# A state-space mixer and its gated unit: lower parts of three tiles and of the first gate weights moved behind the scan, rounded products first

## The chip, the cores and the metric

One core of a Trainium2 chip runs the whole program in one launch. The metric is the device time of one execution in microseconds. TensorE is called PE in the views, VectorE DVE, ScalarE ACT, GpSimd POOL, and SyncE, which only issues DMAs here, SP. PEld is TensorE's weight load.

## What is computed

Two layers of a streaming encoder over 1088 positions of width 1024 (1024 positions of a prompt, 64 of a sample). Layer 0 is attention and a convolutional feed-forward network. Layer 1, which the change touches, is a diagonal complex state-space mixer with a gated unit, and then another such network. Cut to the mixer, with `u` the normed input in blocks of 64 positions:

```python
xr, xi = einsum(u, bbr), einsum(u, bbi)            # 64 groups of 16 channels, 64 complex states each
_, _, sr, si = associative_scan(_affine_combine, (ar, ai, xr, xi), axis=1)
y = einsum(sr, cr) - einsum(si, ci) + d_skip * h
z = jax.nn.gelu(y)
ag = z @ w_glu + b_glu                             # 1024 -> 2048
out = ag[..., :D_MODEL] * jax.nn.sigmoid(ag[..., D_MODEL:])
```

All inputs and outputs are float32. PE multiplies rounded numbers (fp32r), so an exact product is made of three: a matrix `w` is split into a rounded part `hi` and the rest `lo`, the data `z` likewise into `zh` and `zl`, and `hi*zl + hi*zh + lo*zh` is summed in PSUM (`mm3`, L222 to L226).

## The kernel before

**The mixer** (`ssm`, from L1206). The 64 groups are worked on in pairs, numbered q = 0 to 31. A batch holds two of these (q and q+1), except that 0, 1, 30 and 31 stand alone. A batch is a generator, and `staged` runs several of them interleaved, oldest first, so that each engine has the stages of several batches in its queue. One batch does: PE makes `p1`, the input of the scan (L1258); ACT makes the tables `sc` and `rd` (L1266, L1270); DVE multiplies, adds, scans and multiplies again (L1289, L1294, L1295, L1306, L1309, L1310); PE turns the state into outputs in two PSUM banks (L1318, L1324, with one or two filling matmuls of L231 between); ACT copies them to the tile `ys` (L1332) and the end states to `fin` (L1335). The second multiplication, L1310, is the last that DVE does for a batch. PSUM is a pool of its own in the mixer; it is closed behind it, so the first matmul of the gated unit waits for the last `ys` copy, that of q = 31.

Eight q make one tile of 128 channels, kt = 0 to 7. When its last q is copied, `ys` goes to DRAM (L1339) and comes back transposed as `yf` (L1344). ACT then makes `z` with a GELU (L1359, L1362) and its rounded part `zh` in three blocks of columns (L1368: 384, 384 and 320), and DVE makes the lower part `zl` in three instructions (L1372). Each of these stands in its engine's queue between steps of later batches. `ys`, `yf` and `z` share five buffers (`t4`).

**The weights.** `load_unit` loads 128 x 1024 weights into `raw`, of which there are two buffers, and `split_unit` makes `whl`: the rounded part on ACT and the lower part on DVE, both on L217. The gated unit's first two units (weights of m = 0 for both halves of the product) are loaded within the mixer, at the last batch.

**The gated unit** (from L1405). `tile_(m, b)` is one of 8 tiles of output channels and one of 3 blocks of columns. For m = 0 all products of the first six kt (`k0 = KD - 2`) are made for the three blocks, then those of kt = 6, then those of kt = 7, since z of these two comes last. Then ACT takes the sigmoid and DVE the gate. A side job on POOL and DVE (`sums`) prepares weights of the next network.

**The preparation pool.** `prep2` held three tiles of 128 x 1024 during layer 0, `w`, `tl` and `tp`, for tables of the mixer. Nothing uses them in the mixer.

What sets the order on an engine is a scheduler with a model of time, which takes waits into account, and `self.order(x, y)`, by which x comes behind y on its queue. Each queue then runs strictly in that order.

Of the kernel before, what the change touches and what calls it, by code (L numbers as in the profile page):

```python
# [8 lines left out]
F32 = mybir.dt.float32  # L9
F32R = mybir.dt.float32r  # L10
I32 = mybir.dt.int32
AF = mybir.ActivationFunctionType
# [3 lines left out]
P = 128  # L16
D = 1024
KD = 8
SEQ, DEC, PAST = 1024, 64, 512
T = SEQ + DEC  # L20
BLK = [(0, 384), (384, 384), (768, 320)]
# [13 lines left out]
KH = KF // 2  # L35
PRODUCTS = (("a", 0, 0, 0, 0), ("a", 1, 0, 1, 0), ("s", 0, 0, 1, 1), ("s", 0, 1, 0, 1), ("a", 1, 1, 1, 0), ("s", 1, 1, 0, 0), ("s", 1, 0, 1, 1))
SUMMED = (0, 0, 1, 1, 1, 1, 0)
NC_ = 137
NPR = 32

# [3 lines left out]
class Core:  # L44
# [165 lines left out]
        return self.split_unit(raw)  # L210

    behind = ()

    def split_unit(self, raw):
        nc = self.nc
        w = self.big([P, 2, D], "whl")
        x = nc.scalar.activation(w[:, 0], raw, AF.Copy), nc.vector.tensor_sub(w[:, 1], raw, w[:, 0].bitcast(F32))  # L217
        for u, v in zip(x, self.behind):
            self.order(u, v)
        return w  # L220
# [803 lines left out]
    def ssm_chunk(self, q):  # L1024

        nc, a = self.nc, self.a
        G, V = nc.gpsimd, nc.vector
        gs = slice(4 * q, 4 * q + 4)
        if q == 0:
            z = self.pt([P, 8, 112], "z0")  # L1030
# [24 lines left out]
            o = bass.AP(tensor=o.tensor, offset=o.offset, ap=[o.ap[0], [2 * P + 32, 4], [P, 2], [1, 16]])  # L1055
            nc.scalar.activation(o, self.tq[r, gs, 32:64].rearrange("p g (c j) -> p g c j", c=2), AF.Copy)

        w = self.prep2.tile([P, 4, 2, 16, 8], F32, name="w")
        m = self.pm2()
        m = [m[:, i, :512].rearrange("p (g j s) -> p g j s", j=16, s=8) for i in range(2)]  # L1060
        row = lambda x: x[:, :, :, None].to_broadcast([P, 4, 16, 8])
# [6 lines left out]
        for g in range(4):  # L1068
            for c in range(2):
                x = nc.tensor.matmul(kps[:, :P], self.bd_[:, g, c], ct[:, g, c, 0:8].rearrange("p t i -> p (t i)"),  # L1070
                                     start=g + c == 0, stop=g + c == 4)
                self.order(x, behind)
        kt = self.prep.tile([P, P], F32, name="kt")
# [23 lines left out]
    def ssm_toeplitz(self, q):  # L1097

        nc = self.nc
        tl, tp = (self.prep2.tile([P, 8, P], F32, name=x) for x in ("tl", "tp"))  # L1100
        kd = self.kd
        for s in range(8):
            src = bass.AP(tensor=kd.tensor, offset=kd[8 * q * 16:8 * q * 16 + 1, s].offset, ap=[[240, 16], [3840, 8], [1, P]])
            dst = tl.rearrange("(j s) g f -> j s g f", s=8)[:, s]
            nc.sync.dma_start(dst, src)
        nc.scalar.activation(tp.rearrange("p g (i t) -> p g i t", i=16), tl.rearrange("p g (t i) -> p g i t", i=16), AF.Copy)
        nc.sync.dma_start(self.prm[:, 4 * q:4 * q + 4, OKT:OKT + 256], tp.rearrange("p (g e) f -> p g (e f)", e=2))

    def ssm_prep(self):
        self.prep_ctx = self.tc.tile_pool(name="prep", bufs=1)  # L1110
        self.prep = self.prep_ctx.__enter__()
        self.ssm_small()
        yield
        for q in range(8):
            yield from self.ssm_chunk(q)
            yield
            self.ssm_toeplitz(q)
        self.prep_ctx.__exit__(None, None, None)
# [86 lines left out]
    def ssm(self, after):  # L1205
        nc, tc, a = self.nc, self.tc, self.a  # L1206
        off = PPO
        yd = self.dram.tile([D, 8, NC_], F32, name="yd")
        zh, zl = [None] * 3, [None] * 3
        with tc.tile_pool(name="ss", bufs=1) as sp:  # L1210
# [4 lines left out]
            ps = ps_ctx.__enter__()  # L1215
# [31 lines left out]
            def batch(qs):  # L1247
                t, n, e0 = qs[0] // 2, len(qs), qs[0] % 2
# [16 lines left out]
                for c in range(2):  # L1265
                    x = nc.scalar.activation(sc[:, :, c], pm[:, :, OSI:PRM], AF.Copy, scale=(1.0, -1.0)[c])  # L1266
# [5 lines left out]
                        self.order(x, out[0])  # L1272
                if qs[-1] == 31:
                    self.wsrc.pop(0)
                    for j in range(AHEAD):
                        self.load_ahead(1 + j)
                        self.order(self.loaded, got[15])
                if qs[0] == 2:
                    self.order(self.spill(), self.last_u)
                    us.append(self.ssm_load(2))  # L1280
# [16 lines left out]
                for q in qs:  # L1297
                    if q % 4 == 0 and q < 28:
                        k = q // 4 + 1
# [37 lines left out]
                if qs[-1] % 4 == 3:  # L1337
                    kt = qs[-1] // 4
                    out.append(nc.scalar.dma_start(yd[kt * P:kt * P + P].rearrange("(g i) t c -> (i t) g c", i=16), ys[0]))  # L1339
                    yf = self.t4([P, 8, NC_], "yf")  # L1340

                    if kt < 7:
                        yield
                    x = nc.sync.dma_start(yf, yd[kt * P:kt * P + P])  # L1344
                    yfs.append(x)
                    if t + 6 in got:
                        self.order(x, got[t + 6])
                    if kt < 7:
                        yield
                        yield  # L1350
                    if kt == 6:

                        yield
                    if kt == 7:
                        yield
                        yield
                    z = self.t4([P, T], "z")
                    yv = yf.rearrange("p t c -> p c t")
                    x = nc.scalar.activation(z[:, 0:SEQ].rearrange("p (c t) -> p c t", t=8), yv[:, 0:128], AF.Gelu_apprx_tanh)  # L1359
                    self.order(x, out[0])  # L1360
                    self.order(x, out[-1])
                    x = nc.scalar.activation(z[:, SEQ:].rearrange("p (c t) -> p c t", t=8), yv[:, 129:137], AF.Gelu_apprx_tanh)  # L1362
                    self.order(x, out[0])
                    self.order(x, out[-1])
                    for b, (t0, n_) in enumerate(BLK):
                        if kt == 0:
                            zh[b], zl[b] = self.bt(self.blk, b, "zh", F32R), self.bt(self.blk, b, "zl", F32R)
                        nc.scalar.activation(zh[b][:, kt], z[:, t0:t0 + n_], AF.Copy)  # L1368
                    if kt < 7:
                        yield  # L1370
                    for b, (t0, n_) in enumerate(BLK):
                        x = nc.vector.tensor_sub(zl[b][:, kt], z[:, t0:t0 + n_], zh[b][:, kt].bitcast(F32))  # L1372
                        if kt < 7:
                            self.order(x, adds[-1])
            scans, ends = [], []
            self.staged([batch(x) for x in [[0], [1]] + [[q, q + 1] for q in range(2, 30, 2)] + [[30], [31]]], oldest=True)
            self.behind = out[0], ends[-1]
            fo = sp.tile([P, P], F32, name="fo")
            nc.vector.tensor_add(fo, *(fin[:, i].rearrange("p q c s -> p (q c s)") for i in range(2)))
            nc.gpsimd.dma_start(a["o_st"], fo)  # L1380
# [29 lines left out]
        with self.boundary():  # L1410
            def tile_(m, b):
# [6 lines left out]
                    y[b] = self.bt(self.yp, b, "y")  # L1418
                pa, pb = self.mm_ps("pa"), self.mm_ps("pb")

                def products(ks):
                    for ps, w in ((pb, ws[m][1]), (pa, ws[m][0])):
                        for k in ks:
                            self.mm3(ps[:, :n], w, slice(k * P, (k + 1) * P), zh[b][:, k], zl[b][:, k], k == 0, k == KD - 1)
                k0 = 0
                if m == 0:

                    k0 = KD - 2
                    products(range(k0))
                    yield  # L1430
                products(range(k0, KD - 1))
                yield
# [7 lines left out]
                yield  # L1440

            order = [tile_(m, b) for m, b in self.tail_order(KD, 3)]
            for x in order[:3]:
                next(x)
            for x in order[:3] * 2 + [x for x in order[3:] for _ in range(2)]:
                next(x)
# [162 lines left out]
```

## Time and profile before

| | |
|---|---|
| three runs | 2238.83, 2241.77, 2240.37 us; median 2240.37 |
| profiled execution | 2241.03 us, span of the trace 2239.2 us |
| PE busy | 2191.6 us, 98% of the span |
| DVE busy | 1661.3 us, 74% |
| ACT busy | 1042.3 us, 47% |
| granted PE clock, mean | 0.992 |
| mixer, about 1190 to 1294.4 us | PE busy 93 of 104 us |
| gated unit, 1294.4 to 1511 us | PE busy 216.23 of 216.60 us |

A row of the timeline has the start in us from the start of the span, the time the instruction (or several like it) took, engine, line, operation, output and input, size, and how many; in brackets the idle time of the engine before it and what ended that. Instructions of an engine overlap by some tens of nanoseconds, so distances between starts are the better measure of what one costs. A row of the stretches has the stretch, its length, the busy time of PE, PEld, DVE, ACT and POOL with the instructions in brackets, the granted PE clock as a share of full speed, the DMA share and GB/s.

### The profile page before, as it was taken

The page shows a single profiled execution, that of the slowest core. Times are in us where ns is not written, and L with a number is a line of the kernel's source. Part 1 is how long each engine was busy: PE and PEld are TensorE (multiplying, and loading weights), DVE is VectorE, ACT ScalarE, POOL GpSimd, SP SyncE. Part 2 cuts the span into 40 slices and gives each one's busy share as a digit, 9 for nine tenths or more (in the row PEclk, how much of TensorE's full clock was granted, in tenths as well). Part 3 has the DMA queues.
Part 4 walks back from the last instruction along what each step waited for, and adds up shares of the span by engine and source line. Part 5 has one row for each costly group of instructions (what it writes and reads, how often), then busy time and mean ns, then how long its engine had stood idle before and what let it go on. Part 6 is the DMA issues. An engine that isn't in the chain of part 4 may idle for free.

```text
span 2239.2 us, 35982 instructions
## 1 busy us (share of the span) xinstructions
PE 2191.6 (98%) x13875; PEld 2117.1 (95%) x13875; DVE 1661.3 (74%) x2886; ACT 1042.3 (47%) x1890; POOL 412.8 (18%) x474
## 2 busy tenths in 40 slices
PE   9999999999999999999988899999999999999997
PEld 8987789999999999999986699999999999999997
DVE  8687647989878877767758855597976776676764
ACT  5255747422343342555545641263555455455543
POOL 5322004200032423000200034352010110110000
PEclk9999999999999999999999899999999999999999
DMA  5100015655355565887749888752266686579772
GB/s 197 37 22 29 20 62 158 241 188 202 122 150 173 176 208 187 274 279 236 233 163 339 263 280 294 249 167 75 87 224 229 218 297 226 196 272 314 218 253 97
DMA packets 208123, 428.47 MB, mean 191 GB/s; under 512 B 23312, under 2 KB 114224, under 8 KB 205008
## 3 DMA queue, kind: packets, MB, share of 16 engines
q1 hardware_dynamic: 175648, 326.56, 44.2%
q0 software_dynamic: 23984, 95.12, 11.9%
q10 hardware_dynamic: 8320, 4.49, 0.8%
q8 instruction: 109, 1.79, 0.3%
q14 instruction: 62, 0.51, 0.1%
HBM read 297.75 MB, written 128.37 MB: 190 GB/s over the span
## 4 chain that ended last, share of the span: by engine, by line
PE 32%; DMA 13%; DVE 9%; issue 4%; ACT 2%; POOL 2%; SPq 0%; DVEq 0%; ACTq 0%; POOLq 0%
PE mm L224 10%; PE mm L226 10%; PE mm L225 10%; DMA sj<-in_w_up 3%; DMA raw<-in_w_down 2%; DMA jw<-in_w_down 2%; DMA raw<-sd 1%; POOL sj L1391 1%; DMA yd<-ys 1%; DVE whl L217 1%; DMA su<-sj 1%; DMA gd<-t 1%; DVE gt L564 1%; DVE t L425 1%; DMA yf<-yd 1%
## 5 line engine op out<-in xcount | busy, mean ns | idle before, releaser
L224 PE MATMUL mm<-hl,whl 128*128 128x384 f32 (+1 forms) x1960 | 643.3, 329 | 4.1 <-DVE hl L307 3.1
L226 PE MATMUL mm<-hh,whl 128*128 128x384 f32 (+1 forms) x1960 | 641.2, 329 | 2.3 <-DVE whl L217 2.3
L225 PE MATMUL mm<-hh,whl 128*128 128x384 f32 (+1 forms) x1960 | 643.1, 328 | 0.0
L224 PEld LDWEIGHTS mm<-hl,whl 128*128 128x128 f32 x1960 | 368.4, 188 | 6.5 <-DVE hl L307 4.7
L226 PEld LDWEIGHTS mm<-hh,whl 128*128 128x128 f32 x1960 | 368.4, 188 | 3.0 <-DVE whl L217 2.9
L225 PEld LDWEIGHTS mm<-hh,whl 128*128 128x128 f32 x1960 | 368.6, 188 | 0.1
L217 DVE TENSOR_TENSOR whl<-raw,whl 128x1024 fp32r<-128x1024 f32 x202 | 254.9, 1263 | 146.7 <-ACT whl L217 146.2
L217 ACT ACTIVATE whl<-raw 128x1024 fp32r<-128x1024 f32 x202 | 213.0, 1058 | 248.1 <-PE mm L226 128.6
L224 PE MATMUL mm<-gt,whl 128*128 128x384 f32 (+1 forms) x968 | 316.8, 327 | 2.9 <-ACT whl L217 2.4
L226 PE MATMUL mm<-gt,whl 128*128 128x384 f32 (+1 forms) x968 | 315.8, 327 | 0.7 <-DVE whl L217 0.7
L225 PE MATMUL mm<-gt,whl 128*128 128x384 f32 (+1 forms) x968 | 315.9, 327 | 0.0
L224 PEld LDWEIGHTS mm<-gt,whl 128*128 128x128 f32 x968 | 181.7, 188 | 3.7 <-ACT whl L217 2.6
L226 PEld LDWEIGHTS mm<-gt,whl 128*128 128x128 f32 x968 | 181.7, 188 | 1.2 <-DVE whl L217 1.2
L225 PEld LDWEIGHTS mm<-gt,whl 128*128 128x128 f32 x968 | 181.8, 188 | 0.0
L195 DVE TENSOR_TENSOR whl<-raw,whl 128x1024 fp32r<-128x1024 f32 x84 | 96.4, 1154 | 72.7 <-ACT whl L194 71.3
L424 DVE SCALAR_TENSOR_TENSOR t<-u,ppt,t 128x1090 f32<-128x1090 f32 x88 | 126.9, 1443 | 5.8 <-ACT t L423 4.1
L194 ACT ACTIVATE whl<-raw 128x1024 fp32r<-128x1024 f32 x84 | 82.6, 987 | 101.8 <-DMA raw<-sd 40.1
L423 ACT ACTIVATE t<-u,ppt 128x1090 f32<-128x1090 f32 x88 | 114.2, 1298 | 26.2 <-DVE u L520 13.6
L425 DVE SCALAR_TENSOR_TENSOR t<-u,ppt,t 128x1090 f32<-128x1090 f32 x88 | 122.0, 1386 | 0.4
L415 DVE TENSOR_TENSOR u<-rb,mm 128x384 f32<-128x384 f32 (+1 forms) x164 | 80.8, 504 | 31.2 <-PE mm L226 26.4
L438 ACT ACTIVATE t<-t 128x1090 f32<-128x1090 f32 x44 | 49.1, 1115 | 113.1 <-DVE t L425 113.1
L564 DVE TENSOR_TENSOR gt<-gr,gt 128x768 fp32r<-128x768 f32 (+2 forms) x106 | 90.5, 881 | 11.1 <-ACT gt L563 10.2
(389 smaller groups left out, 4141.5 us busy)
## 6 DMA issues: line engine op xcount, KB each, us to landing
raw<-in_w_up SPq DMA_DIRECT2D x88, 512.0 KB, 4.4
raw<-in_w_down SPq DMA_DIRECT2D x74, 512.0 KB, 4.4
raw<-sd SPq DMA_DIRECT2D x40, 512.0 KB, 4.9
sj<-in_w_up POOLq DMA_DIRECT2D x68, 256.0 KB, 6.1
su<-sj POOLq DMA_DIRECT2D x34, 512.0 KB, 5.9
raw<-su SPq DMA_DIRECT2D x34, 512.0 KB, 4.6
pm<-prm SPq DMA_DIRECT2D x32, 522.0 KB, 8.2
gr<-td SPq DMA_DIRECT2D x40, 384.0 KB, 5.6
```

The costliest lines, as they stand in the source:

```text
L194: nc.scalar.activation(w[:, 0], raw, AF.Copy)
L195: nc.vector.tensor_sub(w[:, 1], raw, w[:, 0].bitcast(F32))
L217: x = nc.scalar.activation(w[:, 0], raw, AF.Copy), nc.vector.tensor_sub(w[:, 1], raw, w[:, 0].bitcast(F32))
L224: nc.tensor.matmul(out, w[:, 0, sl], xl, start=start, stop=False, skip_group_check=more)
L225: nc.tensor.matmul(out, w[:, 0, sl], xh, start=False, stop=False, skip_group_check=more)
L226: self.last_mm = nc.tensor.matmul(out, w[:, 1, sl], xh, start=False, stop=stop, skip_group_check=more)
L415: nc.vector.tensor_mul(u[:, t0 + 2:t0 + 2 + np_], rb[:, t0:t0 + np_], ps[:, :np_])
L423: nc.scalar.activation(t, u[:, 0:T + 2], AF.Identity, bias=cb(m), scale=cw(0, m))
L424: nc.vector.scalar_tensor_tensor(t, u[:, 1:T + 3], cw(1, m), t, op0=ALU.mult, op1=ALU.add)
L425: self.last_conv = nc.vector.scalar_tensor_tensor(t, u[:, 2:T + 4], cw(2, m), t, op0=ALU.mult, op1=ALU.add)
L438: nc.scalar.activation(ta, ta, AF.Gelu_apprx_tanh)
L564: nc.vector.tensor_sub(x[:, 1, u], raw, x[:, 0, u].bitcast(F32))
```

## The change

Four edits, all in the mixer and the start of the gated unit.

1. The lower parts `zl` of kt = 3, 4 and 5 are no longer made in the batch. The batch keeps its `z` (`zs[kt] = z`) and ends after `zh`; behind the last batch the nine subtractions are issued, ordered behind the last L1310.
2. The lower parts of the first two units of gate weights are held back (`self.held`) and issued behind the last L1310, ahead of the nine.
3. So that `z` of kt = 4 and 5 can be kept, they don't take one of the five `t4` buffers but one in `prep2` with the tag `p2`, which the preparation's three tiles now share as one tile. The line that makes it is a list comprehension that calls `self.prep2.tile` once for each x, and the tag has one buffer (`bufs=1`): the two z are halves of two different tiles that take turns in one place.
4. For m = 0 the gated unit makes first, for all three blocks and the first six kt, the products `hi*zh` (12 matmuls a block, 36 in all), and in a second pass the other two, `lo*zh` and `hi*zl`. In all later products the order within one kt is `hi*zh`, `lo*zh`, `hi*zl`, where it was `hi*zl`, `hi*zh`, `lo*zh`.

```diff
+LATE = (3, 4, 5)
...
     def split_unit(self, raw):
...
-        x = nc.scalar.activation(w[:, 0], raw, AF.Copy), nc.vector.tensor_sub(w[:, 1], raw, w[:, 0].bitcast(F32))
+        x = [nc.scalar.activation(w[:, 0], raw, AF.Copy)]
+        low = lambda: nc.vector.tensor_sub(w[:, 1], raw, w[:, 0].bitcast(F32))
+        if self.held is not None:
+            self.held.append(low)
+            return w
+        x.append(low())
...
+        self.p2 = self.prep2.tile([P, 3, 1024], F32, name="p2", tag="p2", bufs=1)
...
+                    self.held = held
                     for j in range(AHEAD):
                         self.load_ahead(1 + j)
                         self.order(self.loaded, got[15])
+                    self.held = None
...
-                    z = self.t4([P, T], "z")
+                    if kt == LATE[1]:
+                        late[:] = [self.prep2.tile([P, 2, T], F32, name="z", tag="p2", bufs=1)[:, x] for x in range(2)]
+                    z = late[kt - LATE[1]] if kt in LATE[1:] else self.t4([P, T], "z")
...
+                    if kt in LATE:
+                        zs[kt] = z
+                        return
...
             self.behind = out[0], ends[-1]
+            for low in reversed(held):
+                self.order(low(), ends[-1])
+            for b in range(3):
+                for k, z in zs.items():
+                    self.order(lower(b, k, z), ends[-1])
...
-                def products(ks):
+                def products(ks, of=(0, 1, 2)):
                     for ps, w in ((pb, ws[m][1]), (pa, ws[m][0])):
                         for k in ks:
-                            self.mm3(ps[:, :n], w, slice(k * P, (k + 1) * P), zh[b][:, k], zl[b][:, k], k == 0, k == KD - 1)
+                            for j in of:
+                                e, x = ((0, zh), (1, zh), (0, zl))[j]
+                                nc.tensor.matmul(ps[:, :n], w[:, e, k * P:(k + 1) * P], x[b][:, k], start=k == 0 and j == 0,
+                                                 stop=k == KD - 1 and j == 2)
...
-                    products(range(k0))
+                    products(range(k0), (0,))
+                    yield
+                    products(range(k0), (1, 2))
                     yield
...
-            for x in order[:3]:
+            for x in order[:3] * 2:
                 next(x)
```

On DVE the work moved out of the mixer's tail. This is before, from the last addition of the batch q = 28, 29 to the scan of q = 30 (`wk` is a batch's state, p_12426 the bank of its `p1`):

```order
L1295 TENSOR_TENSOR wk<-wk 128x4x137
L217 TENSOR_TENSOR whl<-raw,whl 128x1024
L1306 SCALAR_TENSOR_TENSOR wk<-rd,wk 128x552
L1372 TENSOR_TENSOR zl<-z,zh 128x384 x2
L1372 TENSOR_TENSOR zl<-z,zh 128x320
L1309 TENSOR_TENSOR wk<-wk,pm 128x552
L1310 TENSOR_TENSOR wk<-wk,sc 128x552
L1289 TENSOR_TENSOR wk<-pm,p_12426 128x2x137
L1294 TENSOR_TENSOR wk<-sc,p_12426 128x2x137
L217 TENSOR_TENSOR whl<-raw,whl 128x1024
L1295 TENSOR_TENSOR wk<-wk 128x2x137
```

And this is the changed DVE queue from the scan of q = 31, the last (lines are shifted: L1316, L1319 and L1320 are the scan and the two multiplications, L220 the lower part of weights, L1395 a `zl`):

```order
L1316 SCALAR_TENSOR_TENSOR wk<-rd,wk 128x276
L1319 TENSOR_TENSOR wk<-wk,pm 128x276
L1320 TENSOR_TENSOR wk<-wk,sc 128x276
L220 TENSOR_TENSOR whl<-raw,whl 128x1024 x2
L1395 TENSOR_TENSOR zl<-z,zh 128x384 x4
L1395 TENSOR_TENSOR zl<-z,zh 128x320 x2
L1395 TENSOR_TENSOR zl<-z,zh 128x384 x2
L1395 TENSOR_TENSOR zl<-z,zh 128x320
L1405 TENSOR_TENSOR fo<-fin 128x128
```

Both weights' lower parts and nine `zl` now stand behind the last multiplication; the first six `zl` are those of kt = 3 and 4, the last three of kt = 5.

On ACT one group moved too. Before, from the write of `ys` of kt = 6; the GELU here is that of kt = 5, and p_12502, p_12542 and p_12562 are output banks of q = 28, 29, of q = 30 and of q = 31:

```order
L1339 DMA yd<-ys 128x8x137
L1359 ACTIVATE z<-yf 128x1024
L1362 ACTIVATE z<-yf 128x64
L1368 ACTIVATE zh<-z 128x384 x2
L1368 ACTIVATE zh<-z 128x320
L1332 ACTIVATE ys<-p_12502 128x2x137
L1332 ACTIVATE ys<-p_12503 128x2x137
L1335 COPY fin<-wk 128x8 x2
L1332 ACTIVATE ys<-p_12542 128x137
L1332 ACTIVATE ys<-p_12543 128x137
L1335 COPY fin<-wk 128x4 x2
L1332 ACTIVATE ys<-p_12562 128x137
```

And in the changed program, where L1342 is the copy to `ys`, L1345 that to `fin`, L1371, L1374 and L1380 are `z` and `zh`, and the banks of q = 28, 29, of q = 30 and of q = 31 are p_12471, p_12508 and p_12528:

```order
L1349 DMA yd<-ys 128x8x137
L1342 ACTIVATE ys<-p_12471 128x2x137
L1342 ACTIVATE ys<-p_12472 128x2x137
L1345 COPY fin<-wk 128x8 x2
L1342 ACTIVATE ys<-p_12508 128x137
L1342 ACTIVATE ys<-p_12509 128x137
L1345 COPY fin<-wk 128x4 x2
L1371 ACTIVATE z<-yf 128x1024
L1374 ACTIVATE z<-yf 128x64
L1380 ACTIVATE zh<-z 128x384 x2
L1380 ACTIVATE zh<-z 128x320
L1342 ACTIVATE ys<-p_12528 128x137
```

`z` and `zh` of kt = 5 moved from ahead of the copies of q = 28 to 30 to between the copies of q = 30 and of q = 31.

PE's queue is the same up to the end of the mixer. The gated unit began with a `hi*zl`; it now begins with the 36 rounded products:

```order
L1452 MATMUL pb<-zh,whl 128x384 x6
L1452 MATMUL pa<-zh,whl 128x384 x6
L1452 MATMUL pb<-zh,whl 128x384 x6
L1452 MATMUL pa<-zh,whl 128x384 x6
L1452 MATMUL pb<-zh,whl 128x320 x6
L1452 MATMUL pa<-zh,whl 128x320 x6
L1452 MATMUL pb<-zh,whl 128x384
L1452 MATMUL pb<-zl,whl 128x384
```

POOL's queue is unchanged. SP's differs in one place: the load of `yf` of kt = 6 now stands ahead of the loads of the gate's third and fourth unit of weights instead of behind them.

More of the change, by code (lines that the diff above doesn't have):

```diff
@@ L212 @@
     behind = ()
+    held = None
     def split_unit(self, raw):
@@ L1056, in ssm_chunk @@
             nc.scalar.activation(o, self.tq[r, gs, 32:64].rearrange("p g (c j) -> p g c j", c=2), AF.Copy)
-        w = self.prep2.tile([P, 4, 2, 16, 8], F32, name="w")
+        w = self.p2[:, 0].rearrange("p (g c j s) -> p g c j s", g=4, c=2, j=16)
         m = self.pm2()
@@ L1099, in ssm_toeplitz @@
         nc = self.nc
-        tl, tp = (self.prep2.tile([P, 8, P], F32, name=x) for x in ("tl", "tp"))
+        tl, tp = (self.p2[:, x].rearrange("p (g f) -> p g f", g=8) for x in (1, 2))
         kd = self.kd
@@ L1368, in batch, with lower @@
                         nc.scalar.activation(zh[b][:, kt], z[:, t0:t0 + n_], AF.Copy)
+                    if kt in LATE:
+                        zs[kt] = z
+                        return
                     if kt < 7:
                         yield
-                    for b, (t0, n_) in enumerate(BLK):
-                        x = nc.vector.tensor_sub(zl[b][:, kt], z[:, t0:t0 + n_], zh[b][:, kt].bitcast(F32))
+                    for b in range(3):
+                        x = lower(b, kt, z)
                         if kt < 7:
                             self.order(x, adds[-1])
+            late, zs, held = [], {}, []
+            def lower(b, k, z):
+                t0, n = BLK[b]
+                return nc.vector.tensor_sub(zl[b][:, k], z[:, t0:t0 + n], zh[b][:, k].bitcast(F32))
             scans, ends = [], []
@@ L1377, in ssm @@
             self.behind = out[0], ends[-1]
+            for low in reversed(held):
+                self.order(low(), ends[-1])
+            for b in range(3):
+                for k, z in zs.items():
+                    self.order(lower(b, k, z), ends[-1])
             fo = sp.tile([P, P], F32, name="fo")
```

## The prediction

> **What bounds the kernel now.** I read the page first, then the waits of PE, then PE's, DVE's and ACT's timelines around 1262 to 1316 us, where every edit lies, and last the granted clock in stretches. The page says that PE is the engine to watch:
>
> ```profile
> span 2239.2 us, 35982 instructions
> PE 2191.6 (98%) x13875; PEld 2117.1 (95%) x13875; DVE 1661.3 (74%) x2886; ACT 1042.3 (47%) x1890; POOL 412.8 (18%) x474
> ```
>
> So whatever shifts PE's start of the gated unit shifts the end, unless a wait behind it absorbs it. The waits of PE from 1261.8 to 1312 us, with the sum, the times and the longest:
>
> ```profile
> PE p L1324 <- DVE wk L1309: 2.4, 2, 2.1
> PE pb L224 <- ACT ys L1332: 0.5, 1, 0.5
> ```
>
> Only the mixer's tail makes PE wait, for DVE, and at its end once for the last `ys` copy. PE's timeline there (128 x 137 groups are the mixer, `pb` is the gated unit):
>
> ```profile
> 1280.66 0.56 PE L231 MATMUL p<-ppt,ident 128*128 128x238 f32 x2
> 1283.29 2.42 PE L1324 MATMUL p<-wk,pm 64*128 64x137 f32 x16 [2.06 <-DVE wk L1309]
> ...
> 1290.48 1.21 PE L1324 MATMUL p<-wk,pm 64*128 64x137 f32 x16
> ...
> 1292.69 1.20 PE L1324 MATMUL p<-wk,pm 64*128 64x137 f32 x16
> 1294.44 0.44 PE L224 MATMUL pb<-zl,whl 128*128 128x384 f32 x1 [0.55 <-ACT ys L1332]
> ...
> 1315.34 0.34 PE L224 MATMUL pb<-zl,whl 128*128 128x384 f32 x1
> ```
>
> The group at 1283.29 takes 2.42 us where equal ones take 1.21: the wait cost a second time. The stretches, each as long as the clock's own step (length, PE, PEld, DVE, ACT, POOL busy, then the granted clock):
>
> ```profile
> 1279.79:1283.20 3.41, 1.44 (x14) 0.88 (x8) 3.38 (x7) 3.41 (x9) 0.00 (x0) 0.99 0.90 259
> 1283.20:1286.62 3.42, 3.33 (x20) 2.91 (x20) 3.39 (x6) 1.88 (x5) 0.22 (x2) 0.50 0.60 170
> 1286.62:1290.03 3.41, 3.41 (x23) 2.93 (x22) 3.13 (x8) 0.88 (x4) 0.19 (x1) 0.52 0.92 296
> 1290.03:1293.44 3.41, 3.41 (x37) 2.67 (x38) 1.91 (x5) 0.64 (x4) 0.00 (x0) 1.00 0.07 27
> ```
>
> A stretch with PE busy for only 1.44 us is followed by two at half clock, 6.8 us. DVE is full meanwhile (3.38 of 3.41). Its timeline with the instructions that move (L217 and L1372) and their neighbours:
>
> ```profile
> 1266.98 0.73 DVE L1295 TENSOR_TENSOR wk<-wk 128x548 f32<-128x548 f32 x1
> 1267.63 1.02 DVE L1372 TENSOR_TENSOR zl<-z,zh 128x384 fp32r<-128x384 f32 x2
> 1268.57 1.30 DVE L1306 TENSOR_TENSOR_SCAN wk<-rd,wk 128x552 f32<-128x552 f32 x1
> 1269.79 0.47 DVE L1372 TENSOR_TENSOR zl<-z,zh 128x320 fp32r<-128x320 f32 x1
> 1270.17 0.73 DVE L1309 TENSOR_TENSOR wk<-wk,pm 128x552 f32<-128x552 f32 x1
> ...
> 1273.04 0.73 DVE L1295 TENSOR_TENSOR wk<-wk 128x548 f32<-128x548 f32 x1
> 1273.87 1.31 DVE L1306 TENSOR_TENSOR_SCAN wk<-rd,wk 128x552 f32<-128x552 f32 x1
> ...
> 1278.74 1.22 DVE L217 TENSOR_TENSOR whl<-raw,whl 128x1024 fp32r<-128x1024 f32 x1
> 1279.88 1.30 DVE L1306 TENSOR_TENSOR_SCAN wk<-rd,wk 128x552 f32<-128x552 f32 x1
> 1281.09 1.40 DVE L1372 TENSOR_TENSOR zl<-z,zh 128x384 fp32r<-128x384 f32 x3
> 1282.41 0.72 DVE L1309 TENSOR_TENSOR wk<-wk,pm 128x552 f32<-128x552 f32 x1
> ...
> 1284.52 1.22 DVE L217 TENSOR_TENSOR whl<-raw,whl 128x1024 fp32r<-128x1024 f32 x1
> 1285.66 0.44 DVE L1295 TENSOR_TENSOR wk<-wk 128x274 f32<-128x274 f32 x1
> ...
> 1289.83 0.53 DVE L1372 TENSOR_TENSOR zl<-z,zh 128x384 fp32r<-128x384 f32 x1
> 1290.28 0.44 DVE L1309 TENSOR_TENSOR wk<-wk,pm 128x276 f32<-128x276 f32 x1
> 1290.63 0.95 DVE L1372 TENSOR_TENSOR zl<-z,zh 128x384 fp32r<-128x384 f32 x2
> 1291.51 0.44 DVE L1310 TENSOR_TENSOR wk<-wk,sc 128x276 f32<-128x276 f32 x1
> ```
>
> **Part 1: the scan chain gets shorter.** From start to start the moved work takes 0.94 + 0.38 (kt = 3), 1.14 and 1.14 (the two weights), 1.32 (kt = 4), 0.45 + 0.88 (kt = 5), together 6.25 us. Not all of it is won. From L1295 to the scan it takes 0.83 us without a filler (1273.04 to 1273.87), and a filler can start after 0.65 (1266.98 to 1267.63): the filler covered 0.18 us of a dependency. Seven places like this, at 0.12 to 0.18 each, make about 1.05. So the last L1310, which ends at 1291.95 (1291.51 + 0.44), will end 5.2 us earlier, at about 1286.75. PE and ACT keep up with that: ACT's tables for the last batches stand ahead of the moved GELU, and PE's wait of 2.06 us and its slow stretch go. PE's last group would start at 1286.8 or a little later, behind PE's own work, and end at about 1288.3.
>
> **Part 2: the GELU of kt = 5 now waits for DVE, and the last copy waits behind it.** This is the step on which the forecast rests. `z` of kt = 5 is a second tile of a tag with one buffer, so it can be written only when `z` of kt = 4 has had its last reader, and that reader is now the sixth `zl` behind the last L1310. The scheduler knows that wait and has put the GELU behind the copies of q = 30, but ahead of those of q = 31. ACT's queue is strict: the copy of q = 31, and with it the closing of the mixer's PSUM on which the first gate matmul waits, is queued behind a GELU that waits for DVE. ACT's rows, for kt = 3 and 5 and the last copy, and two of the tail:
>
> ```profile
> 1261.82 2.05 ACT L1359 ACTIVATE z<-yf 128x1024 f32<-128x1024 f32 x1
> ...
> 1265.17 0.66 ACT L1332 ACTIVATE ys<-p 128x274 f32<-128x274 f32 x2
> ...
> 1281.65 2.04 ACT L1359 ACTIVATE z<-yf 128x1024 f32<-128x1024 f32 x1
> ...
> 1293.92 0.46 ACT L1332 ACTIVATE ys<-p 128x137 f32<-128x137 f32 x2 [1.57 <-PE p L1324]
> ```
>
> ```profile
> 1306.68 1.43 DVE L1372 TENSOR_TENSOR zl<-z,zh 128x384 fp32r<-128x384 f32 x3 [3.25 <-ACT zh L1368]
> ```
>
> The new chain: L1310 ends at 1286.75; two weights at 1.14 make 2.28; six `zl` at 1.32 for three make 2.64 (both from start to start, rows above), with a few hundredths for the end of the last, 1291.7. Then from a GELU to a copy behind its three `zh` it is 3.35 us (1261.82 to 1265.17): the copy starts at 1295.05. From the copy to the first gate matmul it is 0.52 (1293.92 to 1294.44): 1295.6, which is 1.1 us later than the 1294.44 of before. The 5.2 us are won and 6.3 are paid behind them. PE stands still from 1288.3 to 1295.6, some 7.3 us where it stood for 0.55.
>
> **Part 3: the clock.** A gap of 2.06 us within a stretch was enough for half clock; 7.3 us hold at least one whole empty stretch, so the gated unit will start at half clock. How long it stays there, before's trace brackets: 6.8 us behind the gap above, with matmuls of 64 rows, and one step at the start of the kernel, with the dense 128 x 128 ones that the gated unit has too (PE busy 3.17, clock 0.51, and full in the next stretch):
>
> ```profile
> 10.00:13.40 3.40, 3.17 (x10) 3.18 (x11) 3.40 (x7) 2.42 (x5) 0.69 (x1) 0.51 1.05 410
> ```
>
> [...] I take 1.7, from the dense row. [...]
>
> **Part 4: the rest costs nothing.** Rounded products first change no count: 108 matmuls for three blocks either way. They would let PE start without any lower part; but PE is held by the copy of q = 31, at which time the two weights' lower parts and six of the nine `zl` are long made, so this edit wins nothing here. The second pass needs the `zl` of kt = 5 some 6 us after the start of the unit; DVE makes them as soon as ACT has their `zh`, before that start. The tail of z moves with the copy: `zl` of kt = 7 ended at 1308.1 and was used after 1315.34, 7 us of cover, and the delay of both is the same, more so at half clock. SP's load of `yf` of kt = 6 moves ahead of weights that are needed 20 us later; those loads now also wait for `raw`, which the held lower parts free at about 1289 instead of 1285.7, with some 6 us to the ACT rounding that uses them. The prep tile keeps its waits. In the whole gated unit PE is nearly without gaps, so the shift passes through it, and I take it to pass on to the end:
>
> ```profile
> 1294.40:1511.00 216.60, 216.23 (x1312) 215.54 (x1313) 140.71 (x286) 79.94 (x125) 96.57 (x120) 1.00 0.73 252
> ```
>
> **Sum.** 1.1 + 1.7 = 2.8 us against the profiled execution's 2241.03 us: 2243.8. That execution was 0.66 us above the median of the runs, 2240.37; on the median's footing it is 2243.2 us. About 0.2%, 4.5 us, is what a measurement of this kernel can tell from no change, so this counts as the same, on the slow side.
>
> **Rivals.** *The gain comes through* (faster). If the GELU of kt = 5 did not hold the last copy, L1310 at 1286.75 would lead to the last PE group and the unit's start 1.75 us behind that group's start (1292.69 to 1294.44), 1288.6 to 1289: 5.5 us won at full clock, 2234.9. For it speaks that DVE is full and PE waits for it, as read above; against it that ACT's order in the built program has the copy behind that GELU. A version with both z in one tile would do this; the one at hand does not. Chance 0.04.
>
> *Two slow steps* (slower). The restart falls into a step that is already lost and the next one also passes at half clock, as it did after 1283.20: 3.4 us instead of 1.7, and the chain a little longer than the sum of its rows, 1.5 to 2 us, since ACT's GELU and DVE's work run side by side. Together 5 to 5.4, 2245.5. It decides from about 6 us at half clock on. For it is the pair of stretches at 0.50 and 0.52; against it the dense start at one step. Chance 0.2.
>
> *The waits cancel* (no change within 1 us). DVE's bubbles are smaller than I took, L1310 ends 0.8 us earlier, and the clock recovers within 2 us: 2240.9. This is the lower end of my own case and is counted in it.
>
> **How the numbers follow.** My case with its low end has 0.76 and runs from 2240.6 (chain 0.6 shorter, 0.9 lost to the clock) to 2244.8. The range goes to 2245.9 to take in most of the second rival and leaves out the first. Slower by over 0.2% is above 2244.85: the second rival's 0.2 and a little of my case, 0.22. Faster is the first rival and a bit, 0.05. The rest, 0.73, is within 0.2%.
>
> **What would show it.** Right: in the changed profile ACT sits idle ahead of the L1371 GELU of kt = 5 for DVE's L1395, some 5 us; PE's first L1452 is released by ACT's L1342 after a gap near 7 us; the clock stands at 0.5 for 2 to 5 us behind that; the last L1320 ends about 5 us earlier than L1310 did, with the clock at 1.00 before it. Wrong: a gap of under 1 us ahead of L1452 (the first rival), or one of over 10 us (then DVE's chain behind the scan is longer than its rows say), or a half-clock stretch of near 7 us (the second rival), or new waits behind 1312 us.

## The result, and the profile after

The changed kernel takes 2242.1 us in the median of 21 runs (2237.14 to 2248.3), the kernel before, run beside it, 2236.8 in 21 runs (2233.83 to 2243.66). The ratio is 1.002, with a 95% interval of 1.0012 to 1.0027: slower by 2.7 to 6.0 us. Single executions of one kernel lie up to 7 us from their median, so the spans of two profiled executions say nothing of the change (the profiled one of the changed kernel has 2238.57 us, of before 2241.03). What can be compared in them is the distance from one event to another. Below, times "behind the scan" count from the start of the same instruction in each trace, DVE's scan of q = 22, 23: 1262.50 us before, 1258.51 after.

The totals have hardly moved:

```profile
span 2236.5 us, 35985 instructions
PE 2191.7 (98%) x13875; PEld 2118.7 (95%) x13875; DVE 1659.7 (74%) x2886; ACT 1042.6 (47%) x1890; POOL 415.7 (19%) x474
```

All waits of PE in the changed tail, from 1255 to 1312 us, with the sum, the times and the longest:

```profile
PE pb L1452 <- ACT ys L1342: 7.1, 1, 7.1
PE p L238 <- DVE wk L1304: 0.3, 1, 0.3
```

The wait for L1309 of before, 2.4 us in two, is gone. One wait of 7.1 us stands at the start of the gated unit. DVE's rows behind the last scan show what came first:

```profile
1282.41 0.45 DVE L1320 TENSOR_TENSOR wk<-wk,sc 128x276 f32<-128x276 f32 x1
1282.78 2.35 DVE L220 TENSOR_TENSOR whl<-raw,whl 128x1024 fp32r<-128x1024 f32 x2
1285.05 2.76 DVE L1395 TENSOR_TENSOR zl<-z,zh 128x384 fp32r<-128x384 f32 x6
1290.51 1.43 DVE L1395 TENSOR_TENSOR zl<-z,zh 128x384 fp32r<-128x384 f32 x3 [2.71 <-ACT zh L1380]
```

The last L1320 ends 24.35 us behind the scan, where L1310 of before ended at 29.45: 5.1 us won. Then DVE makes two weights and six `zl`, and ACT's queue waits for the sixth:

```profile
1282.40 0.46 ACT L1342 ACTIVATE ys<-p 128x137 f32<-128x137 f32 x2 [1.90 <-PE p L1334]
...
1287.84 2.03 ACT L1371 ACTIVATE z<-yf 128x1024 f32<-128x1024 f32 x1 [4.80 <-DVE zl L1395]
...
1289.97 1.28 ACT L1380 ACTIVATE zh<-z 128x384 fp32r<-128x384 f32 x3
1291.16 0.43 ACT L1342 ACTIVATE ys<-p 128x137 f32<-128x137 f32 x2
```

The copy of q = 30 is at 1282.40; that of q = 31, which PE had ready at about 1284.6, starts at 1291.16, behind the GELU of kt = 5 and its three `zh`. PE's last mixer group and its first matmuls of the gated unit:

```profile
1283.37 1.21 PE L1334 MATMUL p<-wk,pm 64*128 64x137 f32 x16
...
1291.64 2.29 PE L1452 MATMUL pb<-zh,whl 128*128 128x384 f32 x6 [7.07 <-ACT ys L1342]
1293.73 2.12 PE L1452 MATMUL pa<-zh,whl 128*128 128x384 f32 x6
1295.65 1.86 PE L1452 MATMUL pb<-zh,whl 128*128 128x384 f32 x6
1297.35 1.21 PE L1452 MATMUL pa<-zh,whl 128*128 128x384 f32 x6
```

The unit starts 33.13 us behind the scan, 31.94 before: 1.19 later. Six matmuls take 1.9 to 2.3 us until the fourth group, which takes 1.21. The stretches of one clock step each, 3.41 to 3.42 us (length, PE busy, granted clock, DMA share, GB/s), give the reason:

```profile
1283.56:1286.98 3.42, 1.01 (x16) 0.98 0.89 269
1286.98:1290.39 3.41, 0.00 (x0) 0.50 0.52 193
1290.39:1293.80 3.41, 2.16 (x7) 0.50 0.36 109
1293.80:1297.22 3.42, 3.42 (x13) 0.52 0.78 201
1297.22:1300.63 3.41, 3.41 (x23) 1.00 0.86 268
```

The clock is halved from 1286.98 on (0.50 to 0.52) and comes back at 1297.22 (1.00), so the unit's first 5.6 us run at half speed and lose about 2.8 (half of that). Counted from start to start it is a little less: the first 18 matmuls take 5.71 us (1291.64 to 1297.35), in before 3.23 (1294.44 to 1297.67), so 2.5 are lost. Behind 1312 us no wait of PE is new. From its first to its last matmul the gated unit takes 196.14 us, where it took 194.21, and ends 229.27 us behind the scan, 226.15 before: 3.1 us later.

### The profile page after: what moved, and what is told of

Read it like the earlier page. It is cut to its first block, busy times and chain, and to the rows that moved or that the text cites. A ratio compares the mean times of both kernels' runs of the same rounds, so it can differ in the third digit from the quotient of the medians.

```text
span 2236.5 us, 35985 instructions
## 1 busy us (share of the span) xinstructions
PE 2191.7 (98%) x13875; PEld 2118.7 (95%) x13875; DVE 1659.7 (74%) x2886; ACT 1042.6 (47%) x1890; POOL 415.7 (19%) x474
## 4 chain that ended last, share of the span: by engine, by line
PE 82%; DVE 8%; DMA 5%; ACT 2%; issue 2%; SPq 1%; POOL 0%; DVEq 0%; ACTq 0%; POOLq 0%
PE mm L231 21%; PE mm L233 21%; PE mm L232 21%; PE pb L1452 4%; PE pa L1452 4%; PE po L810 2%; PE tps L803 1%; PE sps L780 1%; DMA raw<-in_w_down 1%; DVE whl L220 1%; PE gq L231 1%; PE gq L233 1%; PE gq L232 1%; PE go L231 1%; DVE hl L314 1%
## 5 line engine op out<-in xcount | busy, mean ns | idle before, releaser
L220 DVE TENSOR_TENSOR whl<-raw,whl 128x1024 fp32r<-128x1024 f32 x202 | 253.7, 1258 | 151.0 <-ACT whl L219 150.5
L1452 PE MATMUL pb<-zh,whl 128*128 128x384 f32 (+1 forms) x384 | 96.2, 333 | 7.1 <-ACT ys L1342 7.1
```

The source lines that it names most:

```text
L220: low = lambda: nc.vector.tensor_sub(w[:, 1], raw, w[:, 0].bitcast(F32))
L1452: nc.tensor.matmul(ps[:, :n], w[:, e, k * P:(k + 1) * P], x[b][:, k], start=k == 0 and j == 0, stop=k == KD - 1 and j == 2)
```

## The experiments

Each kernel was timed beside the kernel before, and ratios are to that; its lines are shifted by a few against those above. Theory: the GELU of kt = 5, which waits for DVE because of the one-buffer tag, holds the last `ys` copy, and PE pays for the gap and then at half clock. Rivals: the new order of products costs something itself, or DVE's order behind the scan does.

**Old products.** The gated unit's products as before, the rest as changed.

```diff
...
-                    products(range(k0), (0,))
-                    yield
-                    products(range(k0), (1, 2))
+                    products(range(k0))
...
```

> The changed kernel with the gated unit's products as before: for each kt hi*zl, hi*zh, lo*zh, in one pass. Theory (the rounded products wait for the same copy as any other, so making them first gains and costs nothing): the same as the changed kernel within 0.5 us, ratio 1.002, the gap 7.1 us, no new wait of PE in the unit. Rival A (the order of products costs): faster than the changed kernel by 1 us or more. Rival B (they hide the late lower parts of kt = 5): slower by up to 2 us, with waits of PE for DVE's lower parts in the first 6 us of the unit.

Measured 2240.43 us, ratio 1.002 (1.0011 to 1.0028), a gap of 7.1 us at the same place, start 33.13 us behind the scan and end 229.17. The new order of products neither costs nor wins here: PE isn't held by lower parts but by the copy.

**The nine lower parts ahead of the two weights.**

```diff
-            for low in reversed(held):
-                self.order(low(), ends[-1])
             for b in range(3):
...
+            for low in reversed(held):
+                self.order(low(), ends[-1])
```

> The changed kernel with the nine lower parts ahead of the two weights' lower parts on DVE, behind the last L1320. The one on which the GELU of kt = 5 waits then comes 2.3 us earlier; the scheduler also puts that GELU ahead of the copies of q = 30, which puts about 0.7 us more between it and the last copy. Theory (the chain through that lower part, the GELU and the last copy sets the start): PE's gap shrinks from 7.1 to about 5.5 us, the clock still drops; 1.5 us under the changed kernel if the clock loses the same, ratio about 1.001 to the kernel before. Rival (the first unit's products wait for the weights' lower parts): the gap stays or grows, no gain.

Measured 2238.51 us, ratio 1.0007 (0.9998 to 1.0015). PE's row:

```profile
1288.13 2.29 PE L1452 MATMUL pb<-zh,whl 128*128 128x384 f32 x6 [5.37 <-ACT ys L1342]
```

The gap goes from 7.07 to 5.37 us, the start comes 1.69 us earlier (31.44), since the sixth `zl` no longer waits for the two weights. So the chain runs from DVE through the GELU to PE, and what stands ahead of the sixth `zl` sets the gap. The end, at 226.47, is 2.8 us earlier than in the changed kernel, more than the start: with the gate's matmuls only one step is at half clock. The restart falls 0.45 us into it, in the changed kernel 1.25 us into one; behind the step the clock was 1.00 here and 0.52 there.

```profile
1284.27:1287.68 3.41, 0.00 (x0) 1.00 0.47 155
1287.68:1291.09 3.41, 2.96 (x9) 0.50 0.90 289
1291.09:1294.50 3.41, 3.41 (x21) 1.00 0.74 201
```

The unit loses 1.5 us to it, half of the 2.96, in place of 2.8. Only one execution of each kernel was profiled, so it isn't shown whether the restart meets the same part of a step in the others.

**Filling matmuls in the gap.** Twelve fills of 238 columns behind the last mixer group; their results go nowhere.

```diff
...
+            self.fill(p1s[-1][:, 0, 2 * NC_:], 12, 512 - 2 * NC_, last_p3[0])
```

> The changed kernel with twelve more filling matmuls of 238 columns (about 6 us of PE, on a PSUM bank that nothing uses any more) between its last mixer group and the gated unit. The unit's start is as late as in the changed kernel. Theory (of the loss some 1.2 us are the later start and some 2.8 us the half clock behind the gap): the clock stays at 1.00 there, and the time is 2.8 us under the changed kernel's, 1.2 us above the kernel before (ratio 1.0005). Rival (the clock is no part of it, all is the chain): the same as the changed kernel, ratio 1.002.

Measured 2239.77 us, ratio 1.0015 (1.0003 to 1.0027). The clock was expected to stay at 1.00, and it did not: the fills ended 2.1 us before the unit's first matmul, and a gap of that length was enough for one step at half clock:

```profile
1292.00:1295.40 3.40, 1.34 (x7) 0.98 0.05 19
1295.40:1298.80 3.40, 3.40 (x12) 0.52 0.74 195
1298.80:1302.20 3.40, 3.40 (x23) 1.00 0.76 209
```

The end is at 228.40, 0.9 us earlier than in the changed kernel, with the same start (33.14). That is what one half-speed step less should give (1.1 of the 2.8, half of the 2.16 us of PE's work in that step), but the ratio's interval is too wide to show it, and the clock's full price was not taken away.

**One tile for both z.** The two z become halves of one tile, so the GELU of kt = 5 waits for nobody.

```diff
-                        late[:] = [self.prep2.tile([P, 2, T], F32, name="z", tag="p2", bufs=1)[:, x] for x in range(2)]
+                        z2 = self.prep2.tile([P, 2, T], F32, name="z", tag="p2", bufs=1)
+                        late[:] = [z2[:, x] for x in range(2)]
```

> The changed kernel with z of kt = 4 and 5 as the two halves of one tile of the tag p2, so that the GELU of kt = 5 waits for no lower part; it stands again ahead of the copies of q = 28 to 31. Theory (the GELU waits for the sixth lower part, the last copy waits behind it, and the gap halves the clock): the last L1320 ends as early as in the changed kernel, PE starts the gated unit about 0.6 us behind its last mixer group instead of 7.1 us, at full clock; 5.3 us faster than the kernel before (ratio 0.9976), 9.3 us faster than the changed one. Rival A (the rounded-first products or the new order of products cost the time, not the wait): stays at or above the kernel before, ratio 1.000 to 1.002. Rival B (the lower parts are simply later for the second pass): the gap goes, but PE waits for them some 6 us into the unit, ratio near 1.000.

Measured 2235.53 us, ratio 1.0001 (0.999 to 1.0012). In the tail all came as expected: the start is 26.61 us behind the scan, 5.33 earlier than before, and at full clock. But the time is that of before: by the two ratios the one tile wins some 4 us against the changed kernel, where 9.3 were expected. PE's first matmuls of the unit, and the first `rstd` matmul (the norm behind it, whose squares `sqa` it adds up), where it stands again:

```profile
1291.44 1.31 PE L1453 MATMUL pb<-zh,whl 128*128 128x384 f32 x6 [0.54 <-ACT ys L1342]
...
1445.75 1.44 PE L274 MATMUL pr<-ones,sqa 128*128 128x1 f32 x6 [2.88 <-DVE sqa L268]
```

In before this wait was 0.29 us:

```profile
1446.14 0.83 PE L267 MATMUL pr<-ones,sqa 128*128 128x1 f32 x6 [0.29 <-DVE sqa L261]
```

From within the wait on two steps are at half clock, 0.51 and 0.50, as the stretches of the kernel with one tile show:

```profile
1441.40:1444.80 3.40, 1.47 (x9) 1.00 0.66 270
1444.80:1448.20 3.40, 2.45 (x10) 0.51 0.17 71
1448.20:1451.63 3.43, 3.43 (x12) 0.50 0.00 0
1451.63:1455.00 3.37, 3.37 (x20) 0.99 0.00 0
```

So 2.9 us of wait and about 2.9 of half speed behind it (half of the 2.45 and 3.43 us that PE was busy) take back the 5.3: the unit ends 226.17 us behind the scan, before 226.15. What is late is read from DVE's queue, where the gate and the squares stand behind a piece of the side job (`sums`, which makes the next network's weights) that waits for its load:

```profile
1436.56 0.43 DVE L1422 TENSOR_TENSOR sj<-sj 128x256 f32<-128x256 f32 x1 [4.85 <-DMA sj<-in_w_up]
...
1439.21 0.61 DVE L1469 SCALAR_TENSOR_TENSOR y<-pa,ppt,sg 128x384 f32<-128x384 f32 x1
...
1442.62 0.61 DVE L1469 SCALAR_TENSOR_TENSOR y<-pa,ppt,sg 128x384 f32<-128x384 f32 x1
1444.14 0.96 DVE L264 TENSOR_TENSOR sqa<-sqa 128x768 f32<-128x768 f32 x1 [0.91 <-ACT sqa L262]
1445.14 0.56 DVE L268 TENSOR_TENSOR sqa<-sqa 128x384 f32<-128x384 f32 x1
```

The load of the same piece was waited for in before, too:

```profile
1437.27 0.43 DVE L1395 TENSOR_TENSOR sj<-sj 128x256 f32<-128x256 f32 x1 [4.40 <-DMA sj<-in_w_up]
```

This is a second theory: the side job's loads, not PE, set when the unit's last gates are made, and before was balanced against them to 0.3 us. In the changed kernel, which starts later, PE doesn't wait there at all.

**Fewer pieces of the side job.** With one tile, nine of the next network's units as plain products in place of five leave 26 pieces of 34. That costs PE time later on, so the kernel before with nine is the base.

```diff
-PLAIN = 5
+PLAIN = 9
...
```

> One tile for both z, with the second network's first nine units as plain products in place of five, so that the side job has 26 pieces and not 34 (the price in plain products is in the kernel before with nine, too, to which this is compared). Theory A: the jobs end about 34 us earlier, the first rstd waits under 0.5 us, the unit ends 5.3 us earlier against its scan than in that kernel: 0.9976 of its time. Theory B: the same time as that kernel.

> The kernel before with nine plain units in place of five: the base for the run with the one tile and nine. Four units more in the plain form cost TensorE work in the second network, which both carry. Theory A: the gated unit itself ends where before's does, 226 us behind the scan, within 0.5. Theory B, the side job costs before's unit time already: it ends over 1 us earlier.

Measured 2254.45 us, ratio 1.0073 (1.0057 to 1.0088), and 2262.33, ratio 1.01 (1.0087 to 1.0114). Against each other that is 0.9973, about 0.995 to 0.999 by the two half widths taken together: the one tile is now worth some 6 us, where it was worth nothing with 34 pieces. These are only six runs against five, each set 9 to 11 us wide, so the size is uncertain. The gated unit from first to last matmul (length, then busy PE, PEld, DVE, ACT and POOL, the clock, DMA share and GB/s), first with one tile and 34 pieces:

```profile
1291.44:1491.00 199.56, 196.68 (x1180) 196.31 (x1181) 124.00 (x262) 67.36 (x101) 84.64 (x112) 0.98 0.75 258
```

With one tile and 26:

```profile
1292.33:1486.02 193.69, 193.69 (x1180) 193.64 (x1181) 110.30 (x226) 67.06 (x101) 68.64 (x88) 1.00 0.66 223
```

And the kernel before with 26:

```profile
1295.52:1489.24 193.72, 193.72 (x1180) 193.67 (x1181) 108.05 (x220) 66.97 (x101) 68.64 (x88) 1.00 0.63 217
```

With 26 pieces the unit takes 193.7 us at either start, 30.30 and 33.45 us behind the scan, without a wait at the first `rstd`; with 34 the early start (26.61) stretches it by 5.9. That is what the second theory says. But the profiled pair accounts for only half of the 6 us: its ends are 223.99 and 227.17, 3.2 apart. Behind the unit PE waits 6.5 us for `u` of the second network in the one and 10.2 in the other, which no theory here has. Both starts are late, as ACT waited 5.1 and 5.4 us for a returning `yf` there, so the kernel before with nine missed its expected end (226) by 1.2, and a start as early as 26.61 was not tried with 26 pieces.

**The side job spread.** Every fifth call skipped, with one tile and in the kernel before.

```diff
...
+            calls.append(0)
+            if len(calls) % 5 == 0:
+                return
...
```

> One tile for both z, and the gated unit's side job (the sums of the second network's weights, 34 jobs) skips each fifth call, so that a job starts about every 5.0 us in place of 4.1 and no fifth of VectorE's queue waits for a load. Theory A, the side job paces the unit and took back the 5.3 us: the first rstd matmul waits under 0.5 us (2.88 with the one tile alone), no half clock there, the unit ends 220.8 us behind its scan (226.15 before), time 2231 us, ratio 0.9976. Theory B, the tail's gain is lost for another cause (the half clock, ScalarE's gates, the weights' loads): the wait and the end (226.2) stay, ratio 1.000.

> The kernel before with the same spreading alone, nothing of the change. Theory A: the unit of before was balanced, with 0.29 us of wait at the first rstd, so only that goes: ratio 0.9998 to 1.000. Theory B (the spreading has a worth or a price of its own, in other transfers): 0.998 or 1.002, which would have to be taken off the run with the one tile.

Measured 2268.2 us, ratio 1.0129 (1.0116 to 1.0142), and 2271.62, ratio 1.0148 (1.0133 to 1.0163). Neither theory had this. The pieces now run on past the first `rstd`, whose wait grew to 7.2 and 9.1 us, and into the next network. The edit made late what should have come early; all it tells is that a side job which ends behind that `rstd` makes PE wait there longer. The pair's ratio, 0.9981, doesn't settle anything (about 0.996 to 1.0).

**More room for the loads.** The two z leave 12 KB a partition free in the gated unit. With one tile, three of five loads go there.

```diff
-            x = self.t4([P, 2, 2, 256], "sj")
+            i = (f - PLAIN) * 2 + e
+            k = (0, 1, None, 2, None)[i % 5]
+            x = self.t4([P, 2, 2, 256], "sj") if k is None else sjs[0][:, k].rearrange("p (j c q) -> p j c q", j=2, c=2)
...
+        sjs = [self.prep2.tile([P, 3, 1024], F32, name="sj", tag="p2", bufs=1)]
```

> One tile for both z; of every five of the side job's loads three land in slots of the 12 KB tile that the two z leave free, two in the five shared buffers as before. Theory A1, the loads are late because a load waits for one of the shared buffers: VectorE's waits for loads shrink well under the 51 us of before, the first rstd waits under 1 us (2.88), the unit ends 220.8 to 221.8 us behind its scan (226.2), ratio 0.9976 to 0.998. Theory A2, the transfers themselves or the place of the sums in VectorE's queue keep the pace: waits and end as with the one tile alone, ratio 1.000.

> As the run with more slots, with each piece's sums made three calls behind its load in place of two, some 4 us more for a load to land. Theory A1 or A2 by transfers: the loads have landed when VectorE comes to them, the first rstd waits under 0.5 us, ratio 0.9976. Theory A2 by the place in the queue (the sums stand ahead of the gates whenever they are ready, and the job now ends one call later): the wait at the first rstd stays over 1.5 us, ratio 0.999 to 1.000.

> As the run with more slots, with the side job called in the unit's first six passes, too, so that it starts six calls earlier and ends about six calls (24 us) earlier, ahead of the first rstd. Theory A: no wait there whatever sets the loads' pace, the unit ends 220.8 us behind its scan, time 2231 us, ratio 0.9976. Rival: the early sums stand in VectorE's queue ahead of the last tiles' lower parts and the first weights' , TensorE waits for these by 2 to 5 us in the unit's first 20 us with a half clock behind it, ratio 0.999 to 1.001.

The second of these has `if len(loaded) > 3` for `> 2`, the third a `beside()` in the loop over the first six passes. Measured: 2235.19 us, ratio 0.9993 (0.9983 to 1.0004); 2235.49, 0.9999 (0.9987 to 1.0011); 2236.39, 0.9992 (0.9981 to 1.0003). In none does PE wait at the first `rstd`, and none runs at half clock there (1.00 over the 11 us around it); the rows of the first and the third, one each:

```profile
1447.56 0.72 PE L274 MATMUL pr<-ones,sqa 128*128 128x1 f32 x6
```

```profile
1443.73 0.72 PE L274 MATMUL pr<-ones,sqa 128*128 128x1 f32 x6
```

The ends are 222.94, 225.07 and 222.53 us behind the scan, 3.2, 1.1 and 3.6 earlier than before, not the 5.3 expected. The third starts where one tile alone does (26.62 and 26.61), so this pair of profiles shows best what the side job cost: 3.6 us. The two ratios, whose intervals overlap, are too wide to show it. The first two start later, at 28.02 and 28.16, and in the second PE waits 2.3 us for `zh` of kt = 7. In the third PE waits 0.9 us for the same, as the `yf` of kt = 7 comes back later (its GELU starts 45.8 us behind the scan, 39.9 with one tile alone), and PE's busy time in the unit is 1.0 us over the 193.7. The expected share of VectorE's waits, well under 51 us, came out only partly (45.9 in the first, 35.5 in the third).

**Room from the fourth piece on, and six double calls.** The best of these put together; the sums also stand behind the last `zl` on DVE.

```diff
...
+            for _ in range(2 if len(calls) in (8, 12, 16, 20, 24, 28) else 1):
...
```

> One tile for both z; the side job starts as in the run with the one tile alone (its first three loads in shared buffers, its first sums behind the last tile's lower parts), from the fourth piece on three of five loads go to the free slots, and six of its calls, in the unit's middle, take two pieces, so that it ends some six calls earlier, ahead of the first rstd. Theory A: start 26.6 us behind the scan as with the one tile alone, no wait over 1 us to the unit's end, end at 220.8 to 221.8 (226.2 before), ratio 0.9976 to 0.998. Rival: the denser loads hold VectorE and through the gates the product tiles' PSUM in the middle, the unit ends at 222.5 to 224 as in the runs with more slots, ratio 0.999.

Measured 2240.74 us, ratio 1.0008 (0.9994 to 1.0023): neither theory. PE's waits from 1262 us on:

```profile
PE p L1328 <- ACT ys L1342: 4.5, 1, 4.5
PE pa L1459 <- DVE y L1475: 2.2, 1, 2.2
```

The second is the rival's: denser sums hold the gates, and these the product tiles' PSUM. The first lies in the mixer, ahead of the edit: ACT waits for `yf` of kt = 4, with later copies queued behind that GELU:

```profile
ACT z L1372 <- DMA yf<-yd: 8.2, 2, 6.7
```

With one tile alone, and the same order in ACT's queue there, such waits came to 0.3 us in the profiled execution, with more slots to 3.0. So the start (32.59 us behind the scan) is later by a transfer that was late in this execution, by chance or not, and this run says little of the edit. No version was shown to beat both kernels; the two best, at 0.9993 and 0.9992, can't be told from no change.

The end of the gated unit in the profiled execution, against before's 226.15 us, beside what the ratio makes of 2237 us:

| kernel | end, us | timed, us |
|---|---|---|
| changed | +3.1 | +4.5 (2.7 to 6.0) |
| old products | +3.0 | +4.5 (2.5 to 6.3) |
| filling matmuls | +2.3 | +3.4 (0.7 to 6.0) |
| lower parts first | +0.3 | +1.6 (-0.4 to 3.4) |
| one tile | 0.0 | +0.2 (-2.2 to 2.7) |
| more slots | -3.2 | -1.6 (-3.8 to 0.9) |
| more slots, three calls | -1.1 | -0.2 (-2.9 to 2.5) |
| more slots, early | -3.6 | -1.8 (-4.3 to 0.7) |
| double calls | +4.2 | +1.8 (-1.3 to 5.1) |

Each end lies within its interval, though most intervals are wide, so nothing in this table calls for a cause behind the end of the unit.

## Why the prediction was right, and where it was not

**Part 1, the scan chain.** 5.2 us were forecast, 5.1 measured. The wait for L1309 and its slow stretch went.

**Part 2, the GELU behind DVE.** The step on which the forecast rested came as written: ACT idle for 4.80 us ahead of the GELU (some 5), released by a `zl`; a gap of 7.07 on PE (7.3); a start 1.19 us later (1.1). The run with one tile showed the cause: without the second tile the gap is 0.54 us. The run with the lower parts first showed the chain's other end.

**Part 3, the clock.** This term was mis-sized: 1.7 us taken, half of the dense row's 3.40; 2.8 by the stretches (2.5 by the matmuls' starts), under the 3.4 of the rival. No run shows the 0.9 that the low end of the forecast takes for it: half clock at the head of the gated unit cost 2.8 us in the changed kernel, 1.7 with the filling matmuls (half of 3.40) and 1.5 with the lower parts first. The dense row is one step at half clock at the start of the kernel, where PE restarts at 10.23 us, 0.23 into the step. Here the restart fell 1.25 us into a step, in which PE was then busy for 2.16 of 3.41 us, and the next one, busy throughout, was at half clock (0.52) too; behind that the clock was 1.00. This is the condition of the rival *Two slow steps*, to which I gave 0.2, with the first step in part only; its longer chain did not come: from the last multiplication to the first gate matmul it is 8.78 us, and 8.8 were added up. The half-clock stretch of 5.6 us lies over the 2 to 5 given as a sign of being right and under the near 7 of the rival. Of three half-clock steps with dense 128 x 128 matmuls the one busy for 2.16 us was followed by half clock (0.52), those busy for 2.96 (lower parts first) and 3.17 (the dense row of the prediction) by full clock (1.00). Two others were followed by half clock: the one of 2.45 at the first `rstd` with one tile (0.50 behind it), which has six matmuls of 128 x 1 in it, and one of 3.33 with the mixer's 64-row matmuls (0.52 behind it). So the busy time of a step alone doesn't tell in these traces which clock follows. The steps ahead of three halvings were busy for 1.01, 1.34 and 1.47 us, with 0.50, 0.52 and 0.51 behind them; only with the lower parts first was it an empty one (0.50 behind it).

**Part 4, the rest.** The products in a new order were worth nothing, as said. That "the shift passes through" the gated unit held for a delay, the case at hand: PE met no new wait. It does not hold for a gain, and I had read it from PE's share of busy time alone. That is the failed step in the rival *the gain comes through*, to which I gave 5.5 us: its condition was tried, the start came 5.3 us earlier, and the time stayed where it was, because the side job's loads and a second half-clock stretch took it back. Two things told of this in before's trace: DVE's wait of 4.40 us for a load ahead of the gates, and the 0.29 us of PE at the first `rstd`, a sign of two chains that end together.

**Sum.** 2.8 us were forecast. The unit's end in the profile moved by 3.1: 1.2 from the start and 1.9 from the unit's length. Of the length, 2.5 are lost over the first 18 matmuls and 0.55 are won at the first `rstd`, where before had its own wait of 0.3: the 100 gate matmuls around it take 18.45 us, in before 19.00. The timed 4.5 us (2.7 to 6.0) hold the 3.1, and the forecast 2.8 lies at their lower edge. That the time in us came so close, 2243.2 forecast and 2242.1 measured, is partly luck: the three runs that I started from have a median of 2240.37, 3.6 us above that of all 21, and the loss was larger than forecast, so the two errors cancel. The low end of my case doesn't follow from its terms: a chain 0.6 shorter and 0.9 lost to the clock make 1.4 us, so 2241.8 and not 2240.6.

## What to carry to other kernels

A buffer that is made twice in a comprehension is two buffers that take turns: look at who must let go of it, and what is queued behind the instruction that waits. Before a gain at the head of a stage is booked at its end, look for the place where the busy engine waits next for work that keeps its own pace; a wait of a few tenths there, like the 0.29 us here, can mean that the stage is balanced, and that only a delay passes through. A wait of TensorE can cost as much again behind it: the one of 2.88 us was followed by 5.9 us of matmuls at half clock (0.51 and 0.50), which lost another 2.9.

## What was not expected of the hardware

In the three places shown, a clock step in which PE was busy for 1.01 to 1.47 of its 3.4 us was followed by one at half speed (0.50 to 0.52). Behind half-speed steps in which PE was busy for 2.16 and 2.45 us the clock was 0.52 and 0.50, behind one of 2.96 it was 1.00. The return of a 548 KB tile through memory, with the same instructions in the same order on ACT, kept ACT waiting for 0.3 us in the profile of one kernel (one tile) and 8.2 in that of another (double calls), the start of the gated unit coming 6 us later there (26.61 and 32.59 us behind the scan). With one profile of each, it isn't shown whether this is chance.
